# A list scheduler with other transfer durations and shared waits, 16-row transpositions on 128 rows, and two PSUM banks as one tile each

## The chip, the cores and the metric

The kernel runs on one core of a Trainium2 chip. The metric is the device time of one execution in microseconds, the median of three runs. Five engines share the work: TensorE (PE: matmuls, and transpositions, which are matmuls against an identity), VectorE (DVE), ScalarE (ACT), GpSimd (POOL) and SyncE (SP), which here issues nearly all DMAs. Each engine works its own instructions in a fixed order and waits on semaphores for the others.

## The reference, cut to what matters

One layer of a hybrid encoder in fp32, for a prompt of 512 rows and a sample of 64 rows that share the weights:

```python
xn = _rmsnorm(x, p['ln_mix'])
proj = xn @ p['w_in']
conv_in, z, a, b, qd, kd, vd = jnp.split(proj, SPLIT_AT, axis=-1)
...
g = -jnp.exp(p['a_log']) * jax.nn.softplus(a + p['dt_bias'])
beta = jax.nn.sigmoid(b)
oa, S_new = _gdn_chunked(qa, ka, va, g, beta, S0)       # gated delta rule, 4 heads
...
ob = _diff_attention(qd, k_all, v_all, q_pos, k_pos, lam)   # 4 heads, two softmaxes each
h = x + jnp.concatenate([oa, ob], axis=-1) @ p['w_out']
h = h + _mem_attn(_rmsnorm(h, p['ln_mem_q']), mem_k, mem_v, p['w_mem_q'], p['w_mem_o'])
hn = _rmsnorm(h, p['ln_ffn'])
h = h + jnp.square(jax.nn.relu(hn @ p['w_ff1'])) @ p['w_ff2']
```

The sample group has a cache of 256 rows of keys and values for the diff attention (`cache_diff_k`, `cache_diff_v`), a memory cache (`cache_mem_k`, `cache_mem_v`) and a delta-rule state.

## The kernel before

Every fp32 operand of a large product is split into a high and a low half (`parts`, `split_weights`: a cast on ACT, then a subtraction on DVE), and a product is three matmuls: high by high, low by high, high by low. So `wh`, `wl` are the halves of a weight tile, `raw` the tile as loaded by SP, and a pattern of `wl, wh, wh` runs through PE's order.

The stages are: normalisation and the input projection with the short convolution (to about 100 us), the delta rule in chunks (`gdn_prep`, `gdn_scan`, with PSUM banks `g0` and `g1` for even and odd chunks) beside further projections, the diff attention head by head (`diff_project`, `diff_cache`, `diff_head`) beside them too, then the memory attention (to about 520 us) and the feed-forward products (to 953 us).

PSUM has banks by tag: three `pr` (projections), two `ba`, and one each of `g0`, `g1`, `gs`. `bank(tag)` hands out a new tile each time; the next tile of a tag may be written only when all users of the tile before it are done.

In `diff_project` the keys of one head are split into two stacked pairs of tiles. For the even heads `At0`, `At1` (high and low half of the keys) and `Dt0`, `Dt1` are named so, for the odd heads `kd`, `vb` and `X`, `KQ`. Four DMAs copy rows 64 to 128 of the first pair to both halves of the second pair (`Dt<-At`), and two more then overwrite those rows with rows 0 to 64 (`At<-At`), so the last two must wait until the first four have landed:

```python
for j in range(2):
    for R in (slice(0, 64), slice(64, P)):
        nc.sync.dma_start(second_[j][R], first_[j][64:])
for j in range(2):
    nc.sync.dma_start(first_[j][64:], first_[j][:64])
```

`abT` (tile tag `p0`) holds the projected `a` and `b`, 16 rows by 576 columns, and is turned into `ab2` by five transpositions of 16 rows; from it DVE works out `gg`, the decay of the delta rule, in some 20 short instructions.

No order is written by hand. All instructions are recorded and `arrange` hands them to a list scheduler, `Arrangement`, which simulates the five engines with estimated durations (`Step.cost`, `execute`), takes at each step the instruction that can start first and is most urgent (`choose`), reruns eight times with urgencies taken from the latest allowed starts (`improve`, `latest`), and fixes the order of the best run with links on each engine. Its numbers only set the order; nothing of them is executed. For a DMA they are: when SP is free again, how long one transfer alone takes, and how long one behind others takes.

Of the kernel before, what the change touches and what calls it, by code (L numbers as in the profile page):

```python
# [41 lines left out]
COLD = 9000.0  # L42
BANK_TAGS = ("pr", "ba", "g0", "g1", "gs")
# [48 lines left out]
class Step:  # L92

    def __init__(self, n, inst):
# [4 lines left out]
        self.outs = [Access(ap(x), True) for x in inst.outs if ap(x) is not None]  # L99
        self.before, self.behind, self.after, self.tiles = set(), set(), [], []  # L100
# [9 lines left out]
    def cost(self):  # L110
# [38 lines left out]
class Arrangement:  # L149

    def __init__(self, instructions, homes, closing, opening, chains):
        self.steps = [Step(n, i) for n, i in enumerate(instructions)]
        self.slots, self.home, self.uses = {}, {}, {}
        self.depend(homes, closing, opening, chains)

    def depend(self, homes, closing, opening, chains):
        seen, boundary = {}, None
        for s in self.steps:
# [40 lines left out]
    def run(self):  # L199
# [3 lines left out]
        self.began, self.ran, self.freed, self.handed = {}, {}, {}, []  # L203
        self.opened, self.ended, self.left = {}, {}, {t: len(u) for t, u in self.uses.items()}
        self.place = {t: (k, i) for k, tag in self.slots.items() for i, t in enumerate(tag["tiles"])}
        self.last, self.wire, self.table = (0.0, 0.0), 0.0, None
# [67 lines left out]
    def improve(self, rounds):  # L274
        best = self.run(), self.order
        for _ in range(rounds):
# [3 lines left out]
            best = min(best, (self.run(), self.order), key=lambda b: b[0])  # L280
        return best[1]
# [24 lines left out]
    def open_tiles(self, s):  # L306
        for t in s.tiles:
            if t not in self.opened:
# [5 lines left out]
                if (key, at) in self.freed:  # L314
                    self.handed.append((self.freed[key, at], s))
# [4 lines left out]
    def close_tiles(self, s, end):  # L320
        for t in s.tiles:
            self.left[t] -= 1
            self.ended[t] = max(self.ended.get(t, 0.0), end)
            if self.left[t] == 0:
                tag = self.slots[self.place[t][0]]
                tag["free"].append(self.ended[t])
                self.freed[self.place[t][0], self.ended[t]] = s.n
                self.readmit(tag)

    def start(self, s):  # L330
# [36 lines left out]
def arrange(tc, instructions, homes, chains, closing, opening):  # L367
    for steps in Arrangement(instructions, homes, closing, opening, chains).improve(8).values():
        steps = [s.inst for s in steps if not s.boundary]
        for earlier, later in zip(steps, steps[1:]):  # L370
            tc.add_manual_dep(
                later, earlier.name,
                mybir.DependencyInfo(mybir.DependencyClass.NoSync, mybir.DependencyReason.DATA),
# [5 lines left out]
def hybrid_layer_kernel(  # L379
# [363 lines left out]
    def roots_of(ts):  # L743

        for t in ts:
            n = TT[t][1]
            b = bank("gs")
            if t == 4:
                sides = squares(junk[0][:, : D // 2], folded, P)
                for q in range(2):  # L750
                    mm(b[:DEC, P : P + 1], ident.rearrange("p (t q) -> p q t", q=2)[:, q], sides, start=q == 0, stop=q == 1)
                r1 = root(tiny([P, 1]), n, b[:DEC, P : P + 1])
            else:
                r1 = root(squares(junk[t % 2], xt[t], n), n)
            mm(b[:, :n], bc(r1[:n], [n, P]), ident[:n, :n])
# [7 lines left out]
    keep_busy(4)  # L763
    x4 = small("zr", [P, 320]), small("zr", [P, 320])
# [97 lines left out]
    abT = small("p0", [16, T + DEC])  # L862
    for a0, n in GATHERED:
# [4 lines left out]
        if a0 == 0:  # L868
            scaled(abT[:, :256], b[:16, :256], 0)
            scaled(abT[:, SEQ:T], b[:16, 256:n], 256)  # L870
        else:
            scaled(abT[:, 256:SEQ], b[:16, :n], a0)
    V.tensor_copy(abT[:, T:], abT[:, SEQ:T])
    b = bank()
    for t in range(5):
        tr(b[:, t * 16 : t * 16 + 16], abT[:, t * P : (t + 1) * P])
# [144 lines left out]
    def gdn_prep(c, nb, L):  # L1021
# [9 lines left out]
        def each(f, *args):  # L1031
# [1050 lines left out]
```

## Time and profile before

| | |
|---|---|
| runs | 962.68, 965.38, 965.53 us; median 965.38 us |
| profiled execution | 962.6 us; its span 960.7 us |
| PE busy | 945.8 us (98% of the span), 7028 instructions |
| DVE, ACT, POOL busy | 681.3, 519.9, 63.3 us |
| DMA | 96.08 MB, mean 100 GB/s |
| chain that ended last | PE 92%, DMA 3%, issue 2%, DVE 2%, ACT 1% |

PE is busy nearly all of the time, so the profile is read from PE: where it has nothing to do, where its matmuls follow one another later than their length allows, and where the clock that it was granted is low. The start of a matmul to the start of the next is its step; the duration that a row prints is longer, since matmuls overlap. Times in windows and rows are microseconds from the start of the span.

### The profile page before, as it was taken

How to read it: one execution, taken by the hardware profiler on the slowest of the kernel's cores; microseconds unless marked ns; L12 is line 12 of the kernel's file. 1: busy time of each engine (PE TensorE's matmuls, PEld its weight loads, DVE VectorE, ACT ScalarE, POOL GpSimd, SP SyncE). 2: the span in 40 equal slices, each digit the busy share in tenths (PEclk: the TensorE clock that was granted, in tenths of full speed). 3: DMA queues.
4: the chain of work that ended last, by engine and by line, in shares of the span. 5: the costliest groups of instructions: out<-in, count | busy, mean ns of one | idle time of the engine just before them, and what ended most of it. 6: DMA issues, size and time to landing. Idle time of an engine off the chain costs nothing.

```text
span 960.7 us, 18141 instructions
## 1 busy us (share of the span) xinstructions
PE 945.8 (98%) x7028; PEld 921.8 (96%) x7028; DVE 681.3 (71%) x1528; ACT 519.9 (54%) x1178; POOL 63.3 (7%) x154
## 2 busy tenths in 40 slices
PE   9999999999899999999999999999999999999997
PEld 8999999999799789999999999999999999999996
DVE  5976887887677676655557878557766669877564
ACT  6543674445456675444445568666645545555454
POOL 1641111110010000000000000000000000000000
PEclk9999999999999999999999999999999999999999
DMA  6722322124445666241121423323222233323202
GB/s 199 269 76 71 91 56 56 34 49 137 126 124 138 221 195 195 71 130 45 52 59 45 143 63 104 94 90 91 83 85 89 88 89 88 89 89 89 67 21 99
DMA packets 125523, 96.08 MB, mean 100 GB/s; under 512 B 6226, under 2 KB 112876, under 8 KB 124926
## 3 DMA queue, kind: packets, MB, share of 16 engines
q1 hardware_dynamic: 125070, 94.28, 33.0%
q8 instruction: 55, 0.90, 0.4%
q10 hardware_dynamic: 368, 0.66, 0.2%
q14 instruction: 30, 0.25, 0.1%
HBM read 79.93 MB, written 9.75 MB: 93 GB/s over the span
## 4 chain that ended last, share of the span: by engine, by line
PE 92%; DMA 3%; issue 2%; DVE 2%; ACT 1%; SPq 0%; POOLq 0%; DVEq 0%; POOL 0%
PE pr L471 58%; PE ba L471 12%; PE g L471 11%; PE gs L471 7%; PE ba L475 2%; PE g L475 2%; DMA vb<-vb 1%; DMA Dt<-At 1%; DMA KQ<-vb 1%; DMA u<-in_x_prompt_dram 0%; DMA At<-At 0%; PE gs L475 0%; DVE wl L515 0%; ACT u L560 0%; DVE ta L1467 0%
## 5 line engine op out<-in xcount | busy, mean ns | idle before, releaser
L471 PE MATMUL pr<-u,wh 128*128 128x288 f32 (+2 forms) x1632 | 357.7, 308 | 0.4 <-ACT wh L664 0.2
L471 PEld LDWEIGHTS pr<-u,wh 128*128 128x128 f32 x1632 | 268.6, 190 | 3.3 <-ACT wh L664 0.9
L471 PE MATMUL pr<-u,wl 128*128 128x288 f32 (+2 forms) x816 | 245.5, 306 | 0.0
L471 PEld LDWEIGHTS pr<-u,wl 128*128 128x128 f32 x816 | 153.0, 189 | 0.4
L515 DVE TENSOR_TENSOR wl<-raw,wh 128x1024 fp32r<-128x1024 f32 x65 | 79.7, 1226 | 36.0 <-ACT wh L514 35.7
L471 PE MATMUL pr<-u,w2h 128*128 128x288 f32 x512 | 102.1, 295 | 0.0
L514 ACT CAST wh<-raw 128x1024 fp32r<-128x1024 f32 x65 | 68.1, 1048 | 55.7 <-PE pr L471 43.0
L471 PEld LDWEIGHTS pr<-u,w2h 128*128 128x128 f32 x512 | 81.8, 188 | 0.0
L471 PE MATMUL pr<-f,w2h 128*128 128x288 f32 x384 | 76.5, 295 | 0.0
L471 PE MATMUL pr<-u,w2l 128*128 128x288 f32 x256 | 75.5, 295 | 0.0
L1823 ACT CAST w2h<-r 128x512 fp32r<-128x512 f32 x56 | 34.7, 621 | 61.1 <-PE pr L471 58.2
L471 PEld LDWEIGHTS pr<-f,w2h 128*128 128x128 f32 x384 | 61.4, 188 | 0.0
L471 PE MATMUL pr<-f,w2l 128*128 128x288 f32 x192 | 56.5, 294 | 0.0
L1909 DVE TENSOR_TENSOR u<-u,pr 128x288 f32<-128x288 f32 x96 | 43.1, 449 | 15.0 <-PE pr L471 14.8
L471 PE MATMUL ba<-u,wl 128*128 128x288 f32 x360 | 52.7, 295 | 0.0
L471 PEld LDWEIGHTS ba<-u,wl 128*128 128x128 f32 x360 | 49.4, 188 | 0.0
L471 PEld LDWEIGHTS pr<-u,w2l 128*128 128x128 f32 x256 | 48.0, 188 | 0.0
L1824 DVE TENSOR_TENSOR w2l<-r,w2h 128x512 fp32r<-128x512 f32 x56 | 38.5, 688 | 13.2 <-ACT w2h L1823 12.6
L545 POOL TENSOR_TENSOR tiny<-tiny,nhalf 128x1 f32<-128x1 f32 (+4 forms) x10 | 6.8, 678 | 616.9 <-DVE tiny L1973 509.2
L471 PE MATMUL pr<-wh,u 128*128 128x512 f32 x128 | 44.3, 417 | 0.0
L1589 DVE TENSOR_TENSOR u<-u,pr 128x288 f32<-128x288 f32 (+2 forms) x48 | 21.6, 452 | 20.8 <-PE pr L471 19.4
L471 PEld LDWEIGHTS pr<-f,w2l 128*128 128x128 f32 x192 | 36.0, 188 | 0.0
(532 smaller groups left out, 2021.7 us busy)
## 6 DMA issues: line engine op xcount, KB each, us to landing
raw<-in_w_ff_dram SPq DMA_DIRECT2D x36, 512.0 KB
r<-in_w_ff_dram SPq DMA_DIRECT2D x56, 256.0 KB
raw<-in_w_in_dram SPq DMA_DIRECT2D x27, 512.0 KB
raw<-in_w_mem_k_dram SPq DMA_DIRECT2D x8, 512.0 KB
raw<-in_w_mem_v_dram SPq DMA_DIRECT2D x8, 512.0 KB
raw<-in_w_out_dram SPq DMA_DIRECT2D x8, 512.0 KB
raw<-in_w_mem_q_dram SPq DMA_DIRECT2D x8, 512.0 KB
raw<-in_w_mem_o_dram SPq DMA_DIRECT2D x8, 512.0 KB
```

Of the source, the lines that this page charges most:

```text
L471: nc.tensor.matmul(out, lhsT, rhs, start=start, stop=stop, skip_group_check=skip_group_check)
L475: nc.tensor.transpose(out, in_, ident[:n, :n])
L514: A.copy(wh, raw)
L515: V.tensor_tensor(wl, raw, wh.bitcast(F32), ALU.subtract)
L545: G.tensor_tensor(out, in_, bc(nhalf[: in_.shape[0], 0:1], list(in_.shape)), ALU.pow)
L1589: V.tensor_tensor(hm, hm, b, ALU.add)
L1823: A.copy(wh, src)
L1824: V.tensor_tensor(wl, src, wh.bitcast(F32), ALU.subtract)
L1909: V.tensor_tensor(am, am, b, ALU.add)
```

## The change

1. The scheduler's durations of transfers: one rate by the length of a row (270 to 380 bytes per ns, times 0.6 for transfers of up to 64 partitions with rows from 1024 bytes), a fixed lead of 1600 or 1950 ns, transfers one after another on one wire that starts at 3700 ns, SP taken for 530 ns by an issue (400 before), and SP holding an issue back while more than 2500 ns of transfers are queued.
2. `improve` keeps the priorities of its best run and reruns that at the end.
3. `shared_waits`: of an instruction on PE, ACT or DVE that waits for several others, all but the latest wait are put on earlier instructions of the same engine which wait for nothing themselves.
4. `g0` and `g1` become one tile each; the scheduler tells their uses apart by a number (`turns`), and on the chip only accesses that overlap are ordered.
5. `abT` has 128 rows, zeroed by POOL, and its five transpositions are 128 by 128; the sample's root (`roots_of`, `t == 4`) is one 128-row product with a helper matrix `both_sides` (two DVE additions at the start) and a 128-row broadcast, in place of two products and a broadcast on 64 rows.
6. The one decay matrix of chunk 4 uses a `ba` bank.

```diff
@@ Step.cost, Arrangement.start and execute
-            self.rates = (217.0, 255.0) if row <= 512 else (245.0, 320.0) if row < 2048 else (272.0, 394.0)
+            self.rate = 270.0 if row <= 512 else 300.0 if row < 2048 else 320.0 if row < 4096 else 380.0
+            if row >= 1024 and min(a.dims[0][1] for a in self.ins + self.outs if a.on_chip) <= 64:
+                self.rate *= 0.6
+            self.lead = 1600.0 if self.ins[0].on_chip else 1950.0
...
+        if s.is_dma:
+            at = max(at, self.wire - BACKLOG)
...
-            self.clock[s.engine] = at + 400
-            alone, queued = s.rates
-            self.wire = max(at + 1300 + s.bytes / alone, self.wire + s.bytes / queued)
+            self.clock[s.engine] = at + 530
+            self.wire = max(at + s.lead, self.wire) + s.bytes / s.rate
@@ arrange
-def arrange(tc, instructions, homes, chains, closing, opening):
-    for steps in Arrangement(instructions, homes, closing, opening, chains).improve(8).values():
-        steps = [s.inst for s in steps if not s.boundary]
-        for earlier, later in zip(steps, steps[1:]):
+def arrange(tc, instructions, homes, turns, chains, closing, opening):
+    arrangement = Arrangement(instructions, homes, turns, closing, opening, chains)
+    links = [pair for steps in arrangement.improve(8) for pair in zip(steps, steps[1:])]
+    for kind, pairs in (("NoSync", links), ("Sync", [(p, s) for s, p in arrangement.shared_waits()])):
+        for earlier, later in pairs:
             tc.add_manual_dep(
...
@@ shared_waits (new; the collecting of `need` is left out)
+                for _, m in sorted(need.values(), key=lambda x: self.ran[x[1]])[:-1]:
+                    early = [t for t in idle if self.began[t.n] > self.ran[m] + 150]
+                    if early:
+                        idle.remove(early[-1])
+                        moved.append((early[-1], self.steps[m]))
@@ bank
+    single = {t: ps.tile([P, 512], F32, tag=t, name=t, bufs=1) for t in ("g0", "g1")}
...
     def bank(tag="ba"):
-        return ps.tile([P, 512], F32, tag=tag, name=nm(tag), bufs=BANKS[tag])
+        if tag not in single:
+            return ps.tile([P, 512], F32, tag=tag, name=nm(tag), bufs=BANKS[tag])
+        turns[single[tag].tensor.name].append(len(nc.cur_bb.bb.instructions))
+        return single[tag]
@@ roots_of
-                for q in range(2):
-                    mm(b[:DEC, P : P + 1], ident.rearrange("p (t q) -> p q t", q=2)[:, q], sides, start=q == 0, stop=q == 1)
-                r1 = root(tiny([P, 1]), n, b[:DEC, P : P + 1])
+                mm(b[:, P : P + 1], both_sides, sides)
+                r1 = root(tiny([P, 1]), P, b[:, P : P + 1])
+                mm(b[:, :n], bc(r1, [P, P]), ident.rearrange("p (t q) -> p q t", q=2)[:, 0])
...
+    for q in range(2):
+        one, two = (t.rearrange("p (t q) -> p q t", q=2) for t in (ident, both_sides))
+        V.tensor_tensor(two[:, q], one[:, 0], one[:, 1], ALU.add)
@@ the turn of abT
-    abT = small("p0", [16, T + DEC])
+    abT = small("p0", [P, T + DEC])
+    G.memset(abT, 0.0)
...
-        tr(b[:, t * 16 : t * 16 + 16], abT[:, t * P : (t + 1) * P])
+        tr(b[:, t * 16 : t * 16 + P], abT[:, t * P : (t + 1) * P])
@@ gdn_prep
-            bg = each(mm, lambda i: bc(g_[:, i : i + 1], [P, P]), lambda i: mask)
+            bg = each(mm, lambda i: bc(g_[:, i : i + 1], [P, P]), lambda i: mask, tag="ba" if c == 4 else f"g{c % 2}")
```

The line numbers of the changed kernel are 45 to 50 higher from the helpers on (the matmul helper is L471 before and L516 in it, the transposition L475 and L520). Its order is the old one within a place or two in PE's first 100 us and from 380 us on; it differs in the first 30 us (by up to 26 places) and from 100 to 380 us (by up to 35). Three places:

SP at about 230 us of the span, where the stacked keys of head 0 are copied. Before:

```order
L510 DMA raw_676_3906<-in_w_in_dram 128x8x128
L1635 DMA B0_887_5244<-in_cache_mem_v_dram 128x512
L1383 DMA Dt1_431_2645<-At1_429_2643 64x512 x2
L1410 DMA u_2_76<-in_cache_diff_v_dram 128x2x512
L1383 DMA Dt0_430_2644<-At0_428_2642 64x512 x2
L1383 DMA KQ_513_3066<-vb_511_3064 64x512 x2
L1385 DMA kd_510_3063<-kd_510_3063 64x512
L1406 DMA out_9_dram<-vs_2631 64x128
L1385 DMA At1_429_2643<-At1_429_2643 64x512
L1405 DMA out_3_dram<-u_4_78 128x4x128
L1385 DMA At0_428_2642<-At0_428_2642 64x512
```

After (the two `Dt1<-At1` now stand three rows ahead of these; between them and the first row stand one load of `cache_mem_v` and one of weights):

```order
L1435 DMA At1_330_2548<-At1_330_2548 64x512
L1433 DMA X_404_2961<-kd_402_2959 64x512
L1449 DMA out_2_dram<-p0_343_2658 128x2x128
L1343 DMA out_4_dram<-S_218_1938 128x4x128
L1452 DMA out_8_dram<-p0_343_2658 64x128
L1449 DMA out_2_dram<-p0_346_2700 128x2x128
L1433 DMA Dt0_331_2549<-At0_329_2547 64x512 x2
L1433 DMA X_404_2961<-kd_402_2959 64x512
L1460 DMA u_2_78<-in_cache_diff_v_dram 128x2x512
L1462 DMA p0_359_2785<-in_cache_diff_k_dram 128x512
L1435 DMA At0_329_2547<-At0_329_2547 64x512
```

The copies of `At1` now go out before the four stores, and the weight load, the second `cache_mem_v` load, `KQ` and `kd` moved behind `At0<-At0`; the load of `cache_diff_k` (tile `p0`), which stood four rows ahead of `Dt1`, now stands right ahead of `At0<-At0`.

PE at 241 us, the matmuls ahead of the first one that reads `At0`. Before:

```order
L471 MATMUL pr_600_3500<-u_6_91,wh_598_3496 128x320
L471 MATMUL g1_467_2902<-u_2_76,qz_427_2634 128x256
L471 MATMUL g1_467_2902<-u_4_78,qz_427_2634 128x64
L471 MATMUL pr_600_3500<-u_6_91,wh_598_3496 128x320
L471 MATMUL pr_600_3500<-u_7_92,wl_599_3497 128x320
L471 MATMUL pr_600_3500<-u_7_92,wh_598_3496 128x320 x2
L471 MATMUL pr_600_3500<-u_7_92,wl_599_3497 128x320
L471 MATMUL pr_600_3500<-u_7_92,wh_598_3496 128x320 x2
L471 MATMUL pr_600_3500<-u_7_92,wl_599_3497 128x320
L471 MATMUL pr_600_3500<-u_7_92,wh_598_3496 128x320 x2
L471 MATMUL pr_600_3500<-u_7_92,wl_599_3497 128x320
L471 MATMUL g0_477_2936<-At0_428_2642,qs_425_2632 128x128
```

After:

```order
L520 MATMUL ba_361_2789<-ident_81,p0_359_2785 128x128
L516 MATMUL pr_483_3387<-u_7_94,wh_481_3383 128x320
L520 MATMUL ba_361_2789<-ident_81,p0_359_2785 128x128
L516 MATMUL pr_483_3387<-u_7_94,wl_482_3384 128x320
L520 MATMUL ba_361_2789<-ident_81,p0_359_2785 128x128
L516 MATMUL pr_483_3387<-u_7_94,wh_481_3383 128x320
L520 MATMUL ba_361_2789<-ident_81,p0_359_2785 128x128
L516 MATMUL g0_75<-At0_329_2547,qs_326_2537 128x128
L516 MATMUL g0_75<-At1_330_2548,qs_326_2537 128x128
L516 MATMUL pr_483_3387<-u_7_94,wh_481_3383 128x320
L520 MATMUL ba_362_2796<-ident_81,p1_360_2786 128x128
```

The matmul on `At0` now stands right behind the four transpositions of `cache_diff_k`, and the two matmuls on `qz`, five of the 320-column products (22 stand ahead of it from the start of this weight tile before, 17 now) and four transpositions of the second half of `cache_diff_k` moved behind it.

SP at 305 to 314 us, where the same copies are made for head 3. Before:

```order
L1383 DMA X_674_3904<-kd_672_3902 64x512 x2
L510 DMA raw_768_4371<-in_w_mem_k_dram 128x2x512
L1635 DMA X_884_5241<-in_cache_mem_v_dram 128x512
L1383 DMA KQ_675_3905<-vb_673_3903 64x512 x2
L1385 DMA kd_672_3902<-kd_672_3902 64x512
L1579 DMA u_820_4678<-hd0_122 128x2304
L1579 DMA u_820_4678<-hd1_123 128x2304
L1385 DMA vb_673_3903<-vb_673_3903 64x512
```

After:

```order
L1433 DMA X_548_3782<-kd_546_3780 64x512 x2
L1433 DMA KQ_549_3783<-vb_547_3781 64x512 x2
L1685 DMA X_749_5110<-in_cache_mem_v_dram 128x512
L1435 DMA kd_546_3780<-kd_546_3780 64x512
L1435 DMA vb_547_3781<-vb_547_3781 64x512
L555 DMA raw_633_4240<-in_w_mem_k_dram 128x2x512
L1629 DMA u_685_4547<-hd0_124 128x2304
L1629 DMA u_685_4547<-hd1_125 128x2304
```

The copy `vb<-vb` moved ahead of the two large loads from `hd`, and the weight load behind it.

More of the change, by code (lines that the diff above doesn't have):

```diff
@@ L1 @@
+from bisect import bisect
 from contextlib import ExitStack, contextmanager
@@ L92, with __init__ @@
 class Step:
-    def __init__(self, n, inst):
+    def __init__(self, n, inst, turns):
         self.n, self.inst, self.op = n, inst, str(inst.opcode)
@@ L99, in __init__ @@
         self.outs = [Access(ap(x), True) for x in inst.outs if ap(x) is not None]
+        for a in self.ins + self.outs:
+            if a.tile in turns:
+                a.tile += f".{bisect(turns[a.tile], n)}"
         self.before, self.behind, self.after, self.tiles = set(), set(), [], []
@@ L149, with __init__ @@
 class Arrangement:
-    def __init__(self, instructions, homes, closing, opening, chains):
-        self.steps = [Step(n, i) for n, i in enumerate(instructions)]
+    def __init__(self, instructions, homes, turns, closing, opening, chains):
+        self.steps = [Step(n, i, turns) for n, i in enumerate(instructions)]
         self.slots, self.home, self.uses = {}, {}, {}
@@ L274, in improve @@
     def improve(self, rounds):
-        best = self.run(), self.order
+        best = self.run(), {s.n: s.priority for s in self.steps}
         for _ in range(rounds):
@@ L279, in improve, with shared_waits @@
                     self.steps[n].priority = at
-            best = min(best, (self.run(), self.order), key=lambda b: b[0])
-        return best[1]
+            time = self.run()
+            if time < best[0]:
+                best = time, {s.n: s.priority for s in self.steps}
+        for s in self.steps:
+            s.priority = best[1][s.n]
+        self.run()
+        return [[s for s in steps if not s.boundary] for steps in self.order.values()]
+    def shared_waits(self):
+        index = {s.n: i for steps in self.order.values() for i, s in enumerate(steps)}
+        moved = []
+        for engine in ("PE", "ACT", "DVE"):
+            known, idle = {}, []
+            for s in self.order[engine]:
+                need = {}
+                old = self.follows.get(s.n, set())
+                for m in s.before | old:
+                    p = self.steps[m]
+                    who = (p.engine, m) if p.is_dma else p.engine
+                    if m in index and not p.boundary and (who != engine or m in old) and index[m] > known.get(who, -1):
+                        need[who] = max(need.get(who, (0, 0)), (index[m], m))
+                known.update({who: i for who, (i, m) in need.items()})
+                for _, m in sorted(need.values(), key=lambda x: self.ran[x[1]])[:-1]:
[3 more added lines that the diff above has]
+                        moved.append((early[-1], self.steps[m]))
+                idle = idle[-12:] + ([] if need else [s])
+        return moved
     def tag_in_the_way(self, s):
@@ L314, in open_tiles @@
                 if (key, at) in self.freed:
-                    self.handed.append((self.freed[key, at], s))
+                    last, old = self.freed[key, at]
+                    self.handed.append((last, s))
+                    self.follows.setdefault(s.n, set()).update(self.uses[old])
                 self.opened[t] = at + 33
@@ L1029, in st, with each @@
             return sb(dict(gam="Y", sq="B", eg="B").get(tag, tag) + str(c % 2))[:, :nb]
-        def each(f, *args):
-            b = bank(f"g{c % 2}")
+        def each(f, *args, tag=f"g{c % 2}"):
+            b = bank(tag)
             for i in range(nb):
```

29 lines of the change are left out of this document (16 added, 13 removed).

## The prediction

> **What bounds the kernel now.** I read the page's busy shares first, then the chain of waits, the list of what PE waited for, the same by windows, and last the timelines of PE and SP at the places that these name.
>
> ```profile
> PE 945.8 (98%) x7028; PEld 921.8 (96%) x7028; DVE 681.3 (71%) x1528; ACT 519.9 (54%) x1178; POOL 63.3 (7%) x154
> PE 92%; DMA 3%; issue 2%; DVE 2%; ACT 1%; SPq 0%; POOLq 0%; DVEq 0%; POOL 0%
> PE g L471 <- DMA At<-At: 4.1, 1, 4.1
> PE gs L471 <- POOL ones L499: 1.1, 1, 1.1
> PE g L471 <- DMA vb<-vb: 1.0, 1, 1.0
> PE ba L475 <- DMA u<-in_x_prompt_dram: 0.7, 1, 0.7
> PE ba L471 <- DVE gg L918: 0.3, 1, 0.3
> ```
>
> TensorE is the bound; it stands idle for few microseconds, and the change hardly alters its products. So the gain can come only from places where PE waits, runs at a low clock, or steps slower than its matmuls need. The windows (columns after the window: length, busy time of PE, PEld, DVE, ACT, POOL, then PE's granted clock, DMA share, GB/s) show where these are, and where nothing is to be had:
>
> ```profile
> 110.00:230.00 120.00, 120.00 (x1006) 117.87 (x1006) 98.11 (x248) 65.82 (x149) 19.14 (x39) 1.00 0.21 54
> 243.00:248.00 5.00, 0.93 (x8) 0.69 (x7) 0.71 (x3) 0.37 (x2) 0.00 (x0) 1.00 0.73 183
> 248.10:251.50 3.40, 3.40 (x17) 3.40 (x17) 1.78 (x8) 0.88 (x2) 0.00 (x0) 0.50 0.52 146
> 319.00:322.00 3.00, 2.04 (x14) 1.55 (x12) 1.84 (x7) 1.42 (x5) 0.15 (x1) 1.00 0.86 294
> 520.00:953.00 433.00, 433.00 (x3281) 432.99 (x3280) 308.77 (x590) 245.22 (x527) 0.70 (x1) 1.00 0.28 85
> ```
>
> From 520 to 953 us PE is never idle, and the order there stays as it was: nothing to gain or lose. The time lies at 243 us, at 319 us, and in small pieces before 110 us.
>
> **A: the wait for `At0`.** SP's queue and the chain say how it arises, and PE's timeline what it costs:
>
> ```profile
> 232.53 0.46 SPq L1412 DMA_DIRECT2D p<-in_cache_diff_k_dram  x1
> 234.94 1.21 SPq L1383 DMA_DIRECT2D Dt<-At  x2
> 236.25 0.54 SPq L1410 DMA_DIRECT2D u<-in_cache_diff_v_dram  x1
> 236.89 1.13 SPq L1383 DMA_DIRECT2D Dt<-At  x2
> 237.43 6.67 DMA Dt<-At
> 244.16 3.38 DMA At<-At
> 241.18 0.76 PE L471 MATMUL g<-u,qz 128*128 128x256 f32 x4
> 241.75 0.39 PE L471 MATMUL pr<-u,wh 128*128 128x320 f32 x1
> 243.30 0.31 PE L471 MATMUL pr<-u,wl 128*128 128x320 f32 x1
> 247.68 0.41 PE L471 MATMUL g<-At,qs 128*128 128x128 f32 x2 [4.07 <-DMA At<-At]
> ```
>
> A 320-column matmul steps 0.15 us, so PE stood from 243.45 to 247.68: 4.2 us. `At0<-At0` could be issued only when the second `Dt0<-At0`, on its way for 6.67 us behind loads issued just ahead of it, had landed.
>
> In the new order SP begins with `Dt1<-At1` at about 228 us, since DVE now finishes `At1` ahead of the weight subtraction. I follow the queue from there in the times of before, with 0.55 us for an issue (the rows above) and L for a `Dt<-At` from its issue to landing: the second `Dt1` goes out at 228.8; `At1<-At1` waits until 228.8 + L; then seven issues to the second `Dt0` (3.85 us); `At0<-At0` waits L more and takes 3.4 us. It lands at 236.05 + 2L. L is between 3.4 (the row 244.16, few loads beside it) and 6.67 (the row 237.43, behind three loads). I take 3.4, as now only two loads of 0.75 MB go with the first pair and stores with the second: landing at 242.9.
>
> PE comes to it earlier: five products (0.74 us), the `qz` matmuls (241.18 to 241.75, 0.57) and four transpositions (some 0.11 each, 0.44) have moved behind it, 1.75 us, so at 243.45 - 1.75 = 241.7. The wait left is 1.2. The load of `cache_diff_k`, now queued after `Dt0` and not ahead, can hold PE for about as long at the transpositions just in front, so I take 1.5, with 0 and 8 (at L = 6.67, 249.4 - 241.7) as ends. **Gain 2.7.**
>
> **B: the clock.** After that wait the granted clock is 0.50 for 3.40 us (third window above): 3.4 x 0.5 = 1.7 us lost. The wait at 319 us (0.96 us, row below) brought none: clock 1.00. A remaining wait of 1.5 is nearer to that one. **Gain 1.7**; ends 0 and 1.7. [...]
>
> **C: turns of 16 rows.** Rows from PE's timeline:
>
> ```profile
> 96.80 0.23 PE L475 MATMUL ba<-ident,p 16*128 16x16 f32 x1
> 97.30 0.23 PE L475 MATMUL ba<-ident,p 16*128 16x16 f32 x1
> 97.72 0.27 PE L475 MATMUL ba<-ident,cst 128*6 128x128 f32 x1
> 97.97 0.27 PE L475 MATMUL ba<-ident,cst 128*6 128x128 f32 x1
> 98.83 0.23 PE L475 MATMUL ba<-ident,p 16*128 16x16 f32 x1
> 99.34 0.23 PE L475 MATMUL ba<-ident,p 16*128 16x16 f32 x1
> 99.84 0.23 PE L475 MATMUL ba<-ident,p 16*128 16x16 f32 x1
> 100.26 0.27 PE L475 MATMUL g<-ident,u 128*128 128x128 f32 x1
> ```
>
> One 320-column product stands between two rows each time. A pair with a full transposition takes 0.25 (97.72 to 97.97); the five with 16 rows take 0.50, 0.42, 0.51, 0.50 and 0.42, 2.35 in all, against 5 x 0.25. **Gain 1.1.** Ends 0.9 and 1.2. [...]
>
> What C adds: POOL's memset of 640 columns. POOL is 7% busy and its result is due only at the copies ahead of 96.8 us. Hidden; if POOL were late, ACT's copies and then these turns would be.
>
> **D: `gg`.**
>
> ```profile
> 102.20 1.20 DVE L515 TENSOR_TENSOR wl<-raw,wh 128x1024 fp32r<-128x1024 f32 x1
> 106.52 0.40 PE L471 MATMUL pr<-u,wh 128*128 128x256 f32 x2
> 107.26 0.37 PE L471 MATMUL ba<-gg,triu 128*128 128x20 f32 x2 [0.34 <-DVE gg L918]
> 318.66 0.83 PE L471 MATMUL gs<-u,aT 128*128 128x128 f32 x6
> 320.45 0.33 PE L471 MATMUL g<-vb,qs 128*128 128x128 f32 x1 [0.96 <-DMA vb<-vb]
> 307.53 5.81 DMA KQ<-vb
> 313.40 7.00 DMA vb<-vb
> ```
>
> PE comes to `gg` at 106.76 and starts at 107.26, 0.5 late. DVE's weight subtraction of 1.20 us, now inside the chain that makes `gg`, stands ahead of that chain in the new order, and the matmuls on `gg` stand some 0.9 us later on PE. **Gain 0.6** with the small gaps behind it; ends 0 and 0.8.
>
> **E: the wait for `vb`.** Rows just above: PE is ready at 319.32 (six steps of 0.11 after 318.66) and starts at 320.45, 1.1 late, because `vb<-vb` was issued at 313.40 and went behind two `hd` loads. It now goes ahead of them: `KQ` about a microsecond earlier, 306.7, plus 5.8 and 7.0 at the worst of these rows is 319.5, and without the big loads 3.4 each is 313.5. Even if PE comes 2 us earlier, to 317.3, the wait is gone unless both transfers take their worst. **Gain 1.1**; ends -1 and 1.1. The weight load moved behind `vb` goes out some 4 us later; its product stands after 322 us.
>
> **F: start.**
>
> ```profile
> 17.26 0.40 PE L471 MATMUL gs<-tiny,ident 128*64 128x1 f32 x4
> 19.98 0.32 PE L471 MATMUL gs<-ident,tiny 64*128 64x64 f32 x1
> ```
>
> Four passes (17.26 to 17.59, 0.33) become two, and the 64-row broadcast a full one: 0.3. ACT's and PE's order in the first 15 us also changes; the window 0 to 20 has 2.2 us idle, most of it the first load. I take 0.2 of it; `both_sides` costs DVE about 0.4, beside PE's work. **Gain 0.5**; ends 0 and 1.
>
> **G: shared waits and one tile for `g0` and `g1`.** Both leave the data dependences as they are. Waits that are already met cost PE nothing that shows: 433.00 of 433 us busy with the waits in place. The good end is 0, since full windows leave nothing to gain. On the bad side, a wait put on an earlier instruction by an estimate that is wrong stops PE early; and from 110 to 350 us hundreds of matmuls stand in a new order, where 120.00 of 120 us (110 to 230) were full, so any new gap is a loss. I take **a loss of 1.0**, about the size of one wait like that for `vb`; ends 0 and -3, three such waits.
>
> **Sum:** 2.7 + 1.7 + 1.1 + 0.6 + 1.1 + 0.5 - 1.0 = 6.7 us off the profiled execution of 962.6 (span 960.7): 955.9. The runs before are 0.1, 2.8 and 2.9 above that execution, so the median 965.38 belongs to the upper group; for a median of the kernel after I add 1.1 and forecast **957.0**.
>
> **Rivals.**
> 1. The wait moves to the load of `cache_diff_k`. PE needs it 1 us ahead of `At0`, at 240.7; it goes out at 237.8 behind a load of 0.5 MB. If it takes 6.67, as `Dt` did behind loads, it lands at 244.5: 3.8 us idle, nearly the old wait, and the clock falls again. For it: it was issued five microseconds earlier before. Against: less is queued ahead. A and B shrink to 0.4 and 0: 962.6 - 2.7 + 1.1 = 961.0.
> 2. Slower: SP stands still twice. `At1<-At1` now waits at the head of the queue with stores, loads and `Dt0` behind it. With L = 7.0 (the longest row) `At0` lands at 250.1, 8.4 us late; A becomes -4.2, a second stretch at half clock -1.7, and the weight load behind `At0<-At0`, delayed by as much, costs a further 2 (its cast and subtraction, 2.2 us, no longer hidden). With C to G at +2.3: 962.6 + 5.6 + 1.1 = 969.3. A and G balance at a wait of 6.5, so from L = 6.0 the kernel is slower. Against: only 0.75 MB goes with the first pair, and the second goes with stores.
> 3. The reordering does little: gains of A, B, E and new gaps in 110 to 350 us (3 us, G's end) cancel to what C, D and F give: 962.6 - 2.2 + 1.1 = 961.5 to 963.
>
> **How the numbers follow.** A change below 0.3%, 2.9 us, can't be told from none: faster means below 962.5, slower above 968.3. Forecast 0.62 (all faster); rival 1 0.17, two thirds of it faster; rival 2 0.07; rival 3 0.14, under half of it faster. Faster 0.80, same 0.13, slower 0.07. The range: all terms at their good ends give 962.6 - (4.2 + 1.7 + 1.2 + 0.8 + 1.1 + 1.0) = 952.6, and the low end is put a microsecond below, as runs and profile differ by that and more; upward it takes in rivals 1 and 3, to 963.
>
> **What would show it.** In the profile after: the wait for `At` under 3 us and no 0.50 in the clock near 245 us (A, B); pairs of 0.25 us at the five turns (C); no wait for `gg` or `vb` (D, E). Wrong would be: a wait for `p` before `At`, `At<-At` landing after 246 us, or new rows of PE waiting between 110 and 350 us.

## The result, and the profile after

The kernel after the change took 956.22 us (median of six runs, 955.47 to 956.61), the kernel before, run beside it, 965.24 us (six runs, 962.55 to 965.85). The ratio is 0.9913, with a 95% interval from 0.9898 to 0.9927: 9.0 us or 0.9% faster. The forecast was 957.0. The profiled execution took 955.47 us with a span of 953.8, so against the profiled execution of before (962.6 and 960.7) 7.1 and 6.9 us went; a part of why the medians lie further apart than the two profiled executions is told with the clock, below.

The page's busy shares and chain, and the list of what PE waited for, of the kernel after:

```profile
PE 942.3 (99%) x7026; PEld 919.8 (96%) x7026; DVE 683.7 (72%) x1530; ACT 520.7 (55%) x1178; POOL 62.7 (7%) x155
PE 92%; DVE 3%; issue 2%; POOL 1%; ACT 1%; DMA 0%; POOLq 0%; DVEq 0%; SPq 0%; ACTq 0%
...
PE gs L516 <- POOL ones L544: 1.1, 1, 1.1
PE pr L516 <- DVE wl L560: 0.8, 2, 0.4
PE ba L516 <- DVE gg L968: 0.6, 1, 0.6
```

Two waits are gone, that for `At` (4.1) and that for `vb` (1.0), and DMA's 3% of the chain with them. One is new: `wl`, twice, 0.8 together. The wait for `gg` has not gone; it grew from 0.3 to 0.6. The windows (columns as before) show the stretch after `At` at the full clock:

```profile
110.00:230.00 120.00, 120.00 (x1006) 117.81 (x1007) 98.61 (x249) 61.74 (x144) 17.57 (x36) 1.00 0.22 57
243.00:248.00 5.00, 5.00 (x41) 4.89 (x41) 2.92 (x11) 2.42 (x5) 0.00 (x0) 1.00 0.59 179
```

From 110 to 230 us PE is as full as before, in its new order, and from 513 to 946 us it is busy for 433.00 of 433 us, as it was from 520 to 953.

**Around `At0`**, SP's timeline first, then PE's:

```profile
226.59 1.10 SPq L1433 DMA_DIRECT2D Dt<-At  x2
230.08 0.47 SPq L1435 DMA_DIRECT2D At<-At  x1
233.79 1.11 SPq L1433 DMA_DIRECT2D Dt<-At  x2
236.30 0.43 SPq L1462 DMA_DIRECT2D p<-in_cache_diff_k_dram  x1
236.83 0.47 SPq L1435 DMA_DIRECT2D At<-At  x1
...
241.45 0.27 PE L520 MATMUL ba<-ident,p 128*128 128x128 f32 x1
241.48 0.42 PE L516 MATMUL g<-At,qs 128*128 128x128 f32 x2
```

The product on `At0` follows the transposition ahead of it after 0.03 us. `At0<-At0` goes out 7.3 us earlier than before (236.83, before 244.16) and PE wants it 2.0 us earlier than the 243.45 of before.

**The turns of `abT`, the product on `gg`, and the one on `vb`**, from PE's timeline, with SP's row on the `vb` copy, which now goes out ahead of the `hd` loads (304.07):

```profile
97.58 0.27 PE L520 MATMUL ba<-ident,p 128*128 128x128 f32 x1
...
97.83 0.27 PE L520 MATMUL ba<-ident,p 128*128 128x128 f32 x1
...
107.19 0.31 PE L516 MATMUL pr<-u,wl 128*128 128x320 f32 x1
108.06 0.37 PE L516 MATMUL ba<-gg,triu 128*128 128x20 f32 x2 [0.56 <-DVE gg L968]
...
310.88 0.30 PE L516 MATMUL g<-kd,qs 128*128 128x128 f32 x1
311.02 0.28 PE L516 MATMUL g<-vb,qs 128*128 128x128 f32 x1
...
302.12 0.46 SPq L1435 DMA_DIRECT2D vb<-vb  x1
```

A turn and its product now take 0.25 us (97.58 to 97.83). At `gg` the step from the 320-column product is 0.87 us, of which 0.15 is its own length: 0.72 lost, more than the 0.5 of before. The chain on DVE that makes `gg` starts with a copy, `ab<-ba`. Before, it stood so:

```profile
100.11 0.24 DVE L878 COPY ab<-ba 128x80 f32<-128x80 f32 x1 [0.58 <-PE ba L475]
```

After, the weight subtraction stands ahead of it, and the chain, 100.81 to 107.91 us, has rows that stood outside of it before, three `lev` steps (two of them in the third row here, the other at 102.03) and a copy that stood right behind it:

```profile
99.08 1.21 DVE L560 TENSOR_TENSOR wl<-raw,wh 128x1024 fp32r<-128x1024 f32 x1
100.81 0.22 DVE L928 COPY ab<-ba 128x80 f32<-128x80 f32 x1
102.88 0.60 DVE L1031 SCALAR_TENSOR_TENSOR lev<-X,lev 128x128 f32<-128x128 f32 x2
...
106.65 0.67 DVE L979 COPY p<-ba 6x512 f32<-6x512 f32 x1
```

At `vb` the step is 0.14: nothing lost.

**The new wait for `wl`** needs four engines to be read: POOL, DVE and PE around 52 us, then ACT, DVE and PE around 65 us.

```profile
51.10 0.57 POOL L590 TENSOR_TENSOR tiny<-tiny,nhalf 128x1 f32<-128x1 f32 x1
51.71 1.28 DVE L615 SCALAR_TENSOR_TENSOR u<-u,tiny,gB 128x1024 f32<-128x1024 f32 x1 [3.89 <-POOL tiny L590]
52.91 1.22 DVE L560 TENSOR_TENSOR wl<-raw,wh 128x1024 fp32r<-128x1024 f32 x1
54.18 0.41 PE L516 MATMUL pr<-u,wl 128*128 128x320 f32 x1 [0.43 <-DVE wl L560]
...
63.87 1.28 ACT L1361 ACT_TABLE_LOAD   x1
65.27 1.03 ACT L559 CAST wh<-raw 128x1024 fp32r<-128x1024 f32 x1
66.33 1.22 DVE L560 TENSOR_TENSOR wl<-raw,wh 128x1024 fp32r<-128x1024 f32 x1 [0.78 <-ACT wh L559]
67.61 0.41 PE L516 MATMUL pr<-u,wl 128*128 128x320 f32 x1 [0.37 <-DVE wl L560]
```

At 51 us the root for the memory prompt's normalisation stands on POOL behind some 25 small mask instructions. DVE waits for it for 3.89 us with a weight subtraction queued behind, and PE waits for the subtraction. The load of the memory prompt, which went out at 20.23 us before, goes out at 37.88 in the new order, and the scheduler put the root behind the masks (before, it ran ahead of them, at 28.67 us). At 64 us ACT loads a table (1.28 us) for the two exponentials of `lambda` ahead of a weight cast; the subtraction and PE follow late. The two places cost PE 1.3 us, counted from step to step.

To see where the 6.9 us went, I added up for all rows of PE by how much each step is longer than the usual step of its kind. By this count the sum fell by 6.7 us: from 240 to 260 us by 5.5, from 80 to 100 by 1.1, from 300 to 320 by 0.7, from 260 to 280 by 0.4, in the first 20 us by 0.1; from 100 to 120 us it stayed, and from 40 to 80 it rose by 1.3. The count is an estimate: with other choices of the usual step the fall is between 5 and 7 us, the fall at 240 us and the rise at 40 us stay, and the small pieces move by some tenths. Two matmuls fewer (7026 for 7028) are not in it.

### The profile page after: what moved, and what is told of

Its sections match the earlier page's. It is cut to its first block, busy times and chain, and to the rows that moved or that the text cites. A ratio compares the mean times of both kernels' runs of the same rounds, so it can differ in the third digit from the quotient of the medians.

```text
span 953.8 us, 17996 instructions
## 1 busy us (share of the span) xinstructions
PE 942.3 (99%) x7026; PEld 919.8 (96%) x7026; DVE 683.7 (72%) x1530; ACT 520.7 (55%) x1178; POOL 62.7 (7%) x155
## 4 chain that ended last, share of the span: by engine, by line
PE 92%; DVE 3%; issue 2%; POOL 1%; ACT 1%; DMA 0%; POOLq 0%; DVEq 0%; SPq 0%; ACTq 0%
PE pr L516 56%; PE ba L516 12%; PE g L516 12%; PE gs L516 7%; PE ba L520 3%; PE g L520 2%; DVE p L879 1%; DVE wl L560 1%; DMA u<-in_x_prompt_dram 0%; POOL X L1025 0%; PE gs L520 0%; POOL X L1026 0%; DVE p L683 0%; POOL tiny L590 0%; ACT wh L559 0%
## 5 line engine op out<-in xcount | busy, mean ns | idle before, releaser
L516 PE MATMUL pr<-u,wh 128*128 128x288 f32 (+2 forms) x1632 | 355.8, 307 | 1.0 <-DVE u L786 0.3
L516 PEld LDWEIGHTS pr<-u,wh 128*128 128x128 f32 x1632 | 268.0, 189 | 3.1 <-ACT u L776 1.0
L516 PE MATMUL pr<-u,wl 128*128 128x288 f32 (+2 forms) x816 | 245.8, 307 | 0.8 <-DVE wl L560 0.8
L516 PEld LDWEIGHTS pr<-u,wl 128*128 128x128 f32 x816 | 152.8, 189 | 1.9 <-DVE wl L560 1.2
L516 PE MATMUL pr<-u,w2h 128*128 128x288 f32 x512 | 102.1, 295 | 0.0
L516 PEld LDWEIGHTS pr<-u,w2h 128*128 128x128 f32 x512 | 81.9, 188 | 0.0
L516 PE MATMUL pr<-f,w2h 128*128 128x288 f32 x384 | 76.5, 295 | 0.0
L516 PE MATMUL pr<-u,w2l 128*128 128x288 f32 x256 | 75.5, 295 | 0.0
L516 PEld LDWEIGHTS pr<-f,w2h 128*128 128x128 f32 x384 | 61.4, 188 | 0.0
L516 PE MATMUL pr<-f,w2l 128*128 128x288 f32 x192 | 56.5, 294 | 0.0
L516 PE MATMUL ba<-u,wl 128*128 128x288 f32 x360 | 52.7, 295 | 0.0
L516 PEld LDWEIGHTS ba<-u,wl 128*128 128x128 f32 x360 | 49.4, 188 | 0.0
L590 POOL TENSOR_TENSOR tiny<-tiny,nhalf 128x1 f32<-128x1 f32 (+3 forms) x10 | 7.8, 777 | 619.0 <-DVE tiny L2023 509.2
L516 PEld LDWEIGHTS pr<-u,w2l 128*128 128x128 f32 x256 | 48.0, 188 | 0.0
L516 PE MATMUL pr<-wh,u 128*128 128x512 f32 x128 | 43.5, 416 | 0.0
L516 PEld LDWEIGHTS pr<-f,w2l 128*128 128x128 f32 x192 | 36.0, 188 | 0.0
```

Of the source, the lines that this page charges most:

```text
L516: nc.tensor.matmul(out, lhsT, rhs, start=start, stop=stop, skip_group_check=skip_group_check)
L590: G.tensor_tensor(out, in_, bc(nhalf[: in_.shape[0], 0:1], list(in_.shape)), ALU.pow)
```

## The experiments

In the edits, `put(list, what, where, n)` takes one instruction out of the order that the scheduler settled on for an engine and puts it in n places behind another (0: ahead of it); all else keeps its order. Line numbers then stand 23 to 32 higher. Runs of one group were made on one chip, and each is compared with runs of the kernel before there.

**The wait for `At` and the clock.** Two kernels put the late `At0<-At0` back, by two amounts:

```diff
+    put(sp, at0, kd_copy, 1)                  # e1_at0_late_a: behind kd<-kd
+    put(sp, at0, second_cache_mem_v_load, 1)  # e2_at0_late_b: behind the vb copy and that load
```

> The changed kernel with one row of SP's order moved: the second At<-At copy of head 0 goes out behind the kd copy, some 4.4 us later (about 241.2 instead of 236.8); all else stands as it was. It should land at 243.7 to 244.5, and PE comes to its first reader at 241.5, so PE should idle 2.2 to 3.0 us. Theory (a wait costs its length, and the clock falls only after a longer one, as after the 4.07 us in the profile of before): 956.2 + 2.6 = 958.8, no stretch at half clock. Rival (any wait over about 2 us drops the clock): half clock for some 3.4 us, 1.7 more, 960.5. Rival (the wait for At was not what cost the time): no change, 956.2.

Measured: 958.84 us (958.55 to 960.54), ratio 0.9946 (0.9926 to 0.9967). From the chain, PE's timeline and the windows:

```profile
242.16 2.32 DMA At<-At
...
244.52 0.44 PE L540 MATMUL g<-At,qs 128*128 128x128 f32 x2 [1.84 <-DMA At<-At]
...
246.00:248.00 2.00, 2.00 (x17) 1.95 (x16) 1.02 (x3) 0.99 (x2) 0.00 (x0) 1.00 0.88 257
```

PE waits 1.84 us, the clock stays at 1.00, and the kernel is 2.3 to 2.6 us longer than the kernel after (956.56 and 956.22).

> The same with the row moved further, behind the vb copy and the second cache_mem_v load (about 243.5, behind a weight load of 0.5 MB and one of 0.25 MB). It should land at 247 to 248, PE idle 5.5 to 6.5 us. Theory (its length, and 1.7 for about 3.4 us at half clock): 956.2 + 6.0 + 1.7 = 963.9, and a second group of runs 1 to 3 us higher if the length of the half clock varies from run to run. Rival (the clock has nothing to do with it): 956.2 + 6.0 = 962.2 and a clock of 1.00 in the profile. Rival (the wait is made up later): under 960.

Measured: 964.58 us (963.25 to 966.75), ratio 1.0005 (0.9995 to 1.0015): one transfer moved on SP's queue gives back the whole gain.

```profile
247.55 0.69 PE L540 MATMUL g<-At,qs 128*128 128x128 f32 x2 [5.42 <-DMA At<-At]
...
242.00:247.00 5.00, 0.13 (x2) 0.00 (x0) 0.00 (x0) 0.58 (x1) 0.00 (x0) 0.96 0.87 245
...
253.50:254.00 0.50, 0.50 (x6) 0.50 (x6) 0.50 (x3) 0.00 (x0) 0.00 (x0) 1.00 0.00 0
```

The wait is 5.42 us, and the clock is halved until 253.5 us (the last window above has 1.00 again). The mean of 0.96 over the five microseconds to 247 puts the beginning of the half clock 0.4 us ahead of 247, inside the wait, so it lasted 6.8 us. The step at `At0` and the matmuls at half speed explain the difference: 5.4 + (253.5 - 247.55) / 2 = 8.4, measured 8.0 to 8.4.

**The kernel before once more**, for one profile:

> The kernel before once more, for a second profile of it: its runs fall in two groups, 962.3 to 963.2 and 963.7 to 966.7, and its one profile is of the lower. Theory (the groups differ by how long the clock stays at half after the wait for At): if this run is of the upper group, the stretch at half clock near 248 us is longer than 3.4 us, by about twice the difference of the times. Rival: it is as long, and the difference lies elsewhere, at the start or the end. A run of the lower group would tell nothing.

Measured: 964.61 us, span 962.6, two microseconds above the profiled execution that the prediction was made from.

```profile
248.49 0.66 PE L471 MATMUL g<-At,qs 128*128 128x128 f32 x2 [4.35 <-DMA At<-At]
...
246.00:247.00 1.00, 0.00 (x0) 0.00 (x0) 0.00 (x0) 0.00 (x0) 0.00 (x0) 0.89 0.92 225
...
253.50:254.00 0.50, 0.50 (x7) 0.50 (x6) 0.00 (x0) 0.00 (x0) 0.00 (x0) 0.90 0.00 0
```

Here the half clock begins during the wait (0.89 means 0.22 us at half, so 246.78) and ends at 253.6: 6.8 us, against 3.4 in the first profile, where it began at 248.1. Under matmuls it costs (253.6 - 248.49) / 2 = 2.6 us, and not 1.7. So much the same wait costs 0.9 us more in one execution than in another. That, with the 0.3 us longer wait for `At` and 0.3 for `vb`, is most of the 2.0 us between the two executions. The other 0.5 went in the first 14 us: the half clock of the start (in the first profile a 128x128 transposition steps 0.21 us in it, from 5.68 to 9.04 us, and 0.11 at 10.56) ends at 9.2 us in the first profile and at 11.3 in this one, and the same row of PE (`pr<-u,wl` x8) starts at 26.65 us and at 27.15. All this is a part of why the medians differ by more than the profiles, since the kernel after has no half clock at `At0`. It does have that of the start, which ends at 9.6 us in its first profile and at 11.4 in a second one, with 0.8 us between the two (the same row at 26.19 and 27.01). How many of the timed runs of before had the longer stretch at `At0`, the times alone don't tell.

**Parts 3, 4 and 5 of the change, one at a time.**

```diff
-    for kind, pairs in (("NoSync", links), ("Sync", [(p, s) for s, p in arrangement.shared_waits()])):
+    for kind, pairs in (("NoSync", links), ("Sync", [])):         # e3_no_shared_waits
...
-    single = {t: ps.tile([P, 512], F32, tag=t, name=t, bufs=1) for t in ("g0", "g1")}
+    single, turns = {}, {}                                        # e4_banks_from_pools
...
-        tr(b[:, t * 16 : t * 16 + P], abT[:, t * P : (t + 1) * P])
+        tr(b[:, t * 16 : t * 16 + 16], abT[:, t * P : (t + 1) * P])   # e6_turns_of_16, abT of 16 rows
```

> The changed kernel without its shared waits, the order of every engine unchanged. My term G says that a wait that is already met costs PE nothing that shows: 956.2 within 0.5. [...] Rival (waits put on earlier instructions stop the engine too early): faster, 955 to 955.7.

> The changed kernel with g0 and g1 handed out by the pool as before, the order of every engine unchanged. Theory (the data dependences are the same either way): 956.2 within 0.5. Rival (the hand-over of a bank makes its next writer wait for all readers of the old tile, also of other columns): small gaps at the g0 and g1 matmuls between 110 and 340 us, 0.5 to 2 us slower.

Measured: 956.79 us (955.93 to 957.22), ratio 0.9919 (0.9904 to 0.9933), without the shared waits; 955.23 us (955.06 to 955.81), ratio 0.9905 (0.9889 to 0.9921), with `g0` and `g1` handed out anew each time. Both intervals hold the 0.9913 of the kernel after: neither part has an effect that these runs can tell. The shared waits do take wait instructions away: the traces have 62 on PE's queue with them and 101 without, 213 and 279 on ACT's, 249 and 282 on DVE's. PE's waits for `ones`, `wl` and the first loads are there in all three.

> The changed kernel itself, on the chip of the runs beside it: 956.2 within 0.7 (its six runs were 955.5 to 956.6, in one group), and no stretch at half clock after the first 10 us.

> The changed kernel with abT on 16 rows and its five transpositions of 16 rows again, the order of every engine unchanged. My term C: 1.1 us slower than the changed kernel, 957.3, and pairs of 0.42 to 0.51 us at the five. [...] Rival (the time goes into the wait for gg behind it, 0.56 us in the profile after): 0.5 slower.

Measured on one chip: the kernel after 956.56 us (956.08 to 956.99), ratio 0.9912 (0.9899 to 0.9924); with turns of 16 rows 958.04 us (956.52 to 959.21), ratio 0.9925 (0.9912 to 0.9938). PE's timeline of the latter has the old pairs (the second turn of 16 rows, then two full ones):

```profile
99.66 0.23 PE L520 MATMUL ba<-ident,p 16*128 16x16 f32 x1
100.07 0.27 PE L520 MATMUL ba<-ident,cst 128*6 128x128 f32 x1
100.32 0.27 PE L520 MATMUL ba<-ident,cst 128*6 128x128 f32 x1
```

A pair of 0.41 us (99.66 to 100.07) stands beside a full one of 0.25; the first, from 99.16, took 0.50. The full pair ahead of the next turn of 16 rows is longer too (100.32 to 100.67, 0.35), which my count of pairs left out. From 96 to 102 us PE falls back by 1.2 us against the second profile of the kernel after. The medians differ by 1.5 us, and the runs of the two overlap a little; the rest may be the start, where PE of this profile is 0.7 later at 27 us. So the pairs with 16 rows are longer than the full one by a factor of 1.6 to 2 (0.41 and 0.50 beside 0.25); why, no run shows.

**Part 1, the durations of transfers**, taken out of the kernel after, and put alone into the kernel before:

```diff
-            self.rate = 270.0 if row <= 512 else 300.0 if row < 2048 else 320.0 if row < 4096 else 380.0
+            self.rates = (217.0, 255.0) if row <= 512 else (245.0, 320.0) if row < 2048 else (272.0, 394.0)
...
-            self.clock[s.engine] = at + 530
-            self.wire = max(at + s.lead, self.wire) + s.bytes / s.rate
+            alone, queued = s.rates
+            self.clock[s.engine] = at + 400
+            self.wire = max(at + 1300 + s.bytes / alone, self.wire + s.bytes / queued)
```

> The changed kernel with the old durations of transfers in the scheduler; the rest of the change stays, and the order comes out anew. In it the copies of At1 and of vb still go out early (rows 67 and 117 of SP's order), At0<-At0 three rows later than in the changed kernel, and mem_prompt is loaded early, as before. Theory (the place of these rows makes the time, whatever cost put them there): a wait for At of 0 to 1.5 us and no wait for wl at 54 and 67 us: 955.3 to 957.5. Rival (the new durations are what brings the gain): the wait for At is back, 961 to 964.

Measured: 962.84 us (961.08 to 966.4), ratio 0.9990 (0.9981 to 1.0000). PE's waits, its timeline at the longest, and the window around that:

```profile
PE ba L516 <- DMA p<-in_cache_diff_k_dram: 3.4, 1, 3.4
PE gs L512 <- DVE rB L797: 2.8, 1, 2.8
...
245.34 0.47 PE L516 MATMUL ba<-ident,p 128*128 128x128 f32 x1 [3.41 <-DMA p<-in_cache_diff_k_dram]
...
244.00:248.00 4.00, 2.66 (x12) 2.57 (x12) 0.11 (x1) 0.28 (x1) 0.00 (x0) 0.67 1.01 287
```

The theory (955.3 to 957.5, a wait for `At` at most) missed, and the rival with the durations came true, though not by `At`. This is the first rival of the prediction, in a kernel where it happens: the load of `cache_diff_k` goes out at 240.90 and not at 236.30, PE waits 3.4 us for it, and the clock is at half from 245.3 to 248.7 us (0.67 over 4 us is 2.6 us at half; the window from 248 to 250 has 0.81, another 0.8). A second wait, 2.8 us at 25 us for the `rB` of the start, is new altogether. Together: 3.5 + 1.7 + 3.0 less the 1.3 at `wl`, which this kernel doesn't have, is 6.9 us; measured 6.3 to 6.6.

> The kernel before with the new durations of transfers alone. At1 and At0 and vb go out early in it, and mem_prompt late. Theory: A, B and E are gained (6 to 7 us), C and the 64-row root are not: 957.5 to 959.5. Rival (the early copies need the banks, the waits and the new order of DVE as well): over 962.

Measured: 959.77 us (958.24 to 962.75), ratio 0.9956 (0.9944 to 0.9968), beside 964.17 for the kernel before. A new line in its list of PE's waits:

```profile
PE g L476 <- DMA out_dram<-p: 0.7, 1, 0.7
```

The 959.77 us are a little above the 957.5 to 959.5 of the theory. No wait for `At` or `vb` is left in it, and the clock is at 1.00 from 244 to 252 us; it has the two waits for `wl`, the turns of 16 rows, and, as the line shows, a wait that the profile puts down to a store (the product reads `kd`, whose copy went out at 311.02; which of the two held it stays open). So part 1 alone gives 4.4 us, all but part 1 gives 1.3 (by its interval 0 to 1.8), and all of it 8.0 to 9.0. The parts don't add up: each alone lets the scheduler settle on another order. Parts 2 and 6 were not tried by themselves.

**The row of the `vb` copy.**

```diff
+    put(sp, vb_copy, second_hd_load, 1)   # e10_vb_late
```

> The changed kernel with one row of SP's order moved: vb<-vb of head 3 behind the two hd loads again, as it stood before; all else unchanged. My term E: with 7.0 us for it behind these loads (as in the profile of before) it lands at about 311.5, PE wants it at 311.0, so 0.5 to 1.0 us slower, 957.1 to 957.6. Rival (PE now comes to it late enough): no change, 956.5.

Measured: 963.68 us (961.83 to 964.67), ratio 0.9993 (0.9983 to 1.0004). Every expectation missed: the old row costs 7 us and not one. SP's timeline, the chain, PE's timeline and the window behind it:

```profile
304.56 0.82 SPq L1652 DMA_DIRECT2D u<-hd  x2
...
305.47 10.72 DMA vb<-vb
...
316.24 0.33 PE L539 MATMUL g<-vb,qs 128*128 128x128 f32 x1 [4.56 <-DMA vb<-vb]
...
317.00:319.00 2.00, 2.00 (x8) 1.42 (x6) 0.30 (x2) 1.56 (x3) 0.00 (x0) 0.50 0.04 8
```

In the kernel before, the two `hd` loads of 1.15 MB went out at 309.30 and the `vb` copy landed 11.1 us later (313.40 + 7.00); here they go out at 304.56 and the copy lands 11.6 us later. It was issued 4.1 us behind the loads in the one and 0.9 in the other; so in these two kernels its landing went with the issue of the loads ahead of it, and not with its own. PE came to it at 319.3 before and comes at 311.5 now: 7.8 us sooner, while the loads moved by only 4.7. So the wait of 1.1 becomes 4.7, and behind it the clock is at half for 3.4 us (316.5 to 319.9: it is 0.69 from 316.2 to 317, 0.50 to 319, and 0.77 to 321), which is 1.7 more: 6.4, measured 7.1.

**The losses that the change brought.** One kernel moves the cause of each new wait away:

```diff
+    put(pool, memory_root, fifth_mask_memset, 0)    # the root ahead of most of the masks
+    put(act, exp_lambda, second_next_wh_cast, 1)    # the table load behind two weight casts
+    put(dve, lambda_, second_next_wl, 1)
+    put(dve, each_of_the_lev_steps, gg, 1)          # e7; in e9 further back, behind beta
```

> The changed kernel with three moves in its order, for three waits of PE that the profile after has and my term G and D missed. POOL: the root for mem_prompt goes ahead of the last two mask tiles (DVE waited 3.9 us for it and then made wl late, 0.59 + 0.10 us on PE at 54 us). ACT and DVE: the lambda exponential and what reads it go behind two weight splits (a table load of 1.28 us stood ahead of a split, 0.53 + 0.10 us on PE at 67 us). DVE: the four lev steps go behind gg (0.72 + 0.1 us on PE at 107 us). Theory (each wait goes): 2.1 us faster, 954.1. Rival (PE then waits at the same places for what comes next, the bank copies or the Silu table): 0.5 to 1 faster. Rival (the moved steps come late themselves): same or slower.

Measured: 955.20 us (954.2 to 956.25), ratio 0.9898 (0.9885 to 0.9911), 1.4 us less than the kernel after on the same chip, where the theory had 2.1. Windows of 40 to 80 us, of the kernel after in that group and of this one, then this one's list of waits and PE's timeline:

```profile
40.00:80.00 40.00, 39.20 (x292) 38.80 (x292) 29.75 (x50) 21.81 (x34) 19.46 (x54) 1.00 0.37 109
```

```profile
40.00:80.00 40.00, 40.00 (x302) 40.00 (x301) 31.04 (x53) 22.19 (x36) 22.12 (x54) 1.00 0.41 118
...
PE ba L548 <- DVE p L1027: 0.4, 1, 0.4
...
108.28 0.38 PE L548 MATMUL ba<-gg,triu 128*128 128x2 f32 x2 [0.42 <-DVE p L1027]
```

The waits for `wl` are gone, and PE is full from 40 to 80 us. The wait at `gg` fell from 0.72 to 0.19, but the `lev` steps, moved behind it, now hold up a copy that PE needs next: 0.58 us from step to step. Set beside the first profile of the kernel after, whose start is as long, PE gains 1.3 us by 70 us, loses 0.2 of it at 108, and gives 0.6 back at 365 us, where it now comes too early for a `wl` (a wait of 0.32 in the profile); the span is 953.5 us against 953.8. So the waits at 54 and 67 us have the causes named above, and the 1.4 us between the medians are not all owed to the moves. The second try puts the `lev` steps further back:

> The three moves again, with the four lev steps further behind, after beta and not right after gg (there they held up the copy of the turned gg, and PE waited 0.58 us for that). Theory: that wait goes too; 955.2 of the run before minus 0.5 is 954.7, 1.8 under the changed kernel. Rival (DVE has as much to do either way, and what is put off is late somewhere before 130 us): 955.2 or more.

Measured: 955.47 us (954.67 to 956.11), ratio 0.9907 (0.9895 to 0.9920), no better. The copy is in time, and another one is late:

```profile
PE ba L552 <- DVE kdc L1022: 0.6, 1, 0.6
```

So at 107 us DVE has more to do ahead of PE's next products than fits in the orders tried, and each of them only chose which product waits. The first of the two has the lowest ratio of all, but its interval overlaps that of the kernel after, and the run with `g0` and `g1` handed out anew took 955.23 us.

## Why the prediction was right

The sum came out within half a microsecond of the profiled execution (forecast 955.9, measured 955.5), and the mechanism that carries it, `At0` and its clock, is the one that the first two experiments turn off and on. That it came so close is luck in part: the single terms were off by up to 1.5 us, their errors cancel in part, and another execution of the kernel after, 956.65 us, is further from the first than the first is from the forecast.

- **A, predicted 2.7, measured 4.2.** No wait was left, where 1.5 was expected. The term was mis-sized in two of its numbers. L was taken as 3.4; the rows give 2.9 for `Dt1` (second copy out at 227.1, `At1<-At1` at 230.08) and at most 2.5 for `Dt0` (234.3 to 236.83), and 2.32 and 2.50 are such copies' own times in the first two experiments. And SP began at 226.6, not at 228. `At0` goes out 2.6 us earlier than the 239.45 of the working, lands, by an estimate with 2.5, at 239.3, and is wanted at 241.5.
- **B, predicted 1.7: held.** No half clock near 245 us. In the first experiment the clock stayed at 1.00 behind a wait of 1.84 us, as taken for 1.5.
- **C, predicted 1.1: held.** All pairs are 0.25 to 0.26; undone, 1.2 by the timelines and 1.5 by the medians.
- **D, predicted a gain of 0.6: wrong, a loss of 0.2.** The weight subtraction did leave the chain that makes `gg`. But 1.4 us of other work moved in for its 1.2, a copy of 0.67 us and three `lev` steps of some 0.25 each, so the chain is as long as before (7.1 us, 7.0). And it starts 0.7 us later (100.81, 100.11), though the last turn stands 0.7 us earlier on PE (99.13, 99.84): the subtraction and a copy now stand right ahead of it. It ends 0.8 us later (107.9, 107.1) while PE comes to it 0.6 later; I had counted only what left it. The last experiments show that DVE is short of time there in any order tried.
- **E, predicted 1.1: the wait is gone, and all losses from 300 to 320 us together shrank by 0.7.** The price of the old row was taken as a property of the row, 1.1 us; in the new order it is 7. The bad end, -1, allowed for a second late transfer, not for the clock.
- **F, predicted 0.5: between 0.1 and 0.5, not settled.** The wait for `ones`, 1.1 us, stayed, and steps in the first 20 us shrank by 0.1, but that count leaves out the passes that are gone. The row of PE at 26.65 us (26.19 after) is 0.46 earlier in the first two profiles and 0.14 in the second two (27.15, 27.01), and the start of one kernel alone varies by more.
- **G, predicted a loss of 1.0: 1.3, in another place.** I had looked for it in the shared waits and in the reordered stretch from 110 to 350 us. Taking the shared waits out changed nothing, and that stretch has no new gap worth a microsecond. The loss lies at 54 and 67 us, where PE's own order hardly differs: the scheduler moved a load by 17.7 us, with it a root on POOL, and a table load on ACT, and both reach PE over two engines that work in order.

Of the rivals, the first (the wait moves to `cache_diff_k`) didn't happen here but in the kernel with the old durations, at 3.4 us where 3.8 was worked out. The second (`At0` so late that all is lost) is what the second experiment made: at 5.4 us of wait the gain is gone, where the working had put the balance at 6.5. Its longer half clock (3.0 us lost under matmuls, where 1.7 was taken) is one reason, and C to G gave less than the 2.3 us that they were counted at. The third (the reordering cancels the gains) has nothing for it but the 1.3 us of G and 0.2 of D.

## What to carry to other kernels

Price a late transfer as the wait, plus half of whatever time the clock then stays at half under matmuls: here 1.84 us of wait with the clock at 1.00 came to 2.3 to 2.6 us, and 5.42 us with the clock at half for 6.8 us, 6.0 of them under matmuls, to 8.0 to 8.4. When an upstream wait goes, ask of each later transfer whether it moves forward by as much: the copy behind the two big loads landed 11.1 and 11.6 us after their issue, whether it was issued 4.1 us behind them or 0.9, and so a row that cost 1 us before cost 7. When a scheduler reorders, look for the loss where other engines changed, not where the bound engine did, and count what has moved into a chain as well as what has left it.

## What the runs showed of the hardware

In these traces the half clock in the middle of the kernel lasted 3.4 us or twice that. It was 3.413 us in the first profile of the kernel before (from 248.10 us; wait 4.07), 3.4 with the old durations (wait 3.41), 3.41 with the late `vb` (wait 4.56, 316.5 to 319.9), and 6.8 in the second profile of before (wait 4.35) and with the later `At0` (wait 5.42). Where it was 6.8, it began during the wait; where it was 3.4, it began as the wait ended or up to 0.4 us later. The length of the wait alone doesn't decide: 4.35 gave the long one, 4.56 the short one. What does, no run shows. The stretches at full clock were whole multiples of the 3.413 us in the first profiles of the two kernels, up to rounding: 238.933 us (9.169 to 248.102) before, 70 of them, and 938.665 us (9.629 to 948.294) after, 275. Where the changes lie in the span differs from one execution to the next: the half clock of the start ended at 9.2 and 11.3 us in the two profiles of before, at 9.6 and 11.4 in those of the kernel after.

The clock was at 1.00 after a wait of 0.96 us (`vb` in the first profile of before, window 319 to 322) and after one of 1.84 us (first experiment, windows from 244 to 252). After the 2.84 us with the old durations (the wait that ends at 28.66) PE's steps show the full clock too: eight 320-column products from 29.29 us take 1.33 us, and eight such take 1.34 in the first profile of before (26.65 us). With the waits of 3.41 us and more in the list above it went to half. Between 2.84 and 3.41 us the traces show nothing.

A 128 KB copy from SBUF to SBUF took 2.3 us (`At0` in the first experiment) and 2.5 (a `KQ<-vb` in the second) where no load went out in the two microseconds ahead of it, 3.4 (`At0` before, behind a store of 256 KB) and 3.5 (`At0` in the second experiment, right behind a load of 256 KB), 5.8, 6.7 and 7.0 behind loads in the profile of before, and 10.7 behind 2816 KB. I had taken the 3.4 as the time alone.
